# The normalization of six mLSTM heads traced one step later and kept together on VectorE, two blocks scaled at a time

## Chip, cores and metric

The kernel runs on one core of a Trainium2 chip. The core has five engines with a queue of instructions each: TensorE (matmuls; PE in the profile), VectorE (DVE), ScalarE (ACT), GpSimd (POOL) and SyncE (SP), which here only issues DMAs. The metric is the device time of one execution in microseconds (us). The times come from repeated executions, the profile from one more.

## The reference, cut to what matters

The program is a model of two layers in fp32, 512 tokens by 1024 features: dilated window attention and a feed-forward block, then an mLSTM mixer and a feed-forward block, then a last RMS norm. The change lies in the mLSTM mixer. The reference computes it in chunks of 64 tokens:

```python
def mlstm_chunk_step(carry, xs):
    ...
    sm = w_intra * jnp.einsum('bhtd,bhsd->bhts', q, k)
    num = jnp.einsum('bhts,bhsv->bhtv', sm, v) + w_inter[..., None] * jnp.einsum('bhtd,bhdv->bhtv', q, C)
    den = jnp.sum(sm, axis=-1) + w_inter * jnp.einsum('bhtd,bhd->bht', q, n)
    h = num / jnp.maximum(jnp.abs(den), jnp.exp(-m_t))[..., None]
    ...

def mlstm_mixer(xn, w_in, conv_w, conv_b, ig_bias, fg_bias, head_gain, w_out):
    proj = xn @ w_in
    ...
    h = h * lax.rsqrt(jnp.mean(h * h, axis=-1, keepdims=True) + RMS_EPS)
    h = h.reshape(B, S, D_MODEL).astype(xn.dtype) * head_gain.astype(xn.dtype)
    return (h * jax.nn.sigmoid(o_pre)) @ w_out
```

There are 8 heads with keys of 64 and values of 128 features. Each head's output is divided by its denominator, normalized over its 128 features, multiplied by a gain and a gate, and projected.

## The kernel before, in words

**Products.** Weights are fp32 and every projection is done as three matmuls of a high and a low part (`SPLITS`). A chunk of weights, 128 x 1024 values, is loaded by SP into one of three buffers, its high part is made by ScalarE (L209) and its low part by VectorE (L210), each into one of three buffers. `project` takes two chunks for 256 output columns: for each, two times 12 matmuls of 128x512 (L240), in the order high-high, high-low, low-high, so that the third matmul needs the low part. After the second chunk the `evac` of each half runs. `project_tokens` does the same for the values, with 48 matmuls of 128x256 a chunk (L272).

**Steps.** After every chunk `advance()` raises a counter and runs what was deferred to that step (`at_tick`, `defer`; within a step in the order in which it was deferred, that is by head). Counted from `base`, the steps of the mLSTM stage are: 1 to 4 the first values, 5 and 6 query/key columns 0, 7 and 8 columns 2, 9 and 10 values of pair 2, 11 and 12 columns 1, 13 and 14 columns 3, 15 and 16 values of pair 3, and 17 to 24 the four output-gate projections `mo0` to `mo3`. Each query/key projection ends with two evictions `pre` (L1312) and is followed by `convolve`, two chains of four VectorE operations (L1319, L1321) and a Silu.

**Heads.** `HEAD_AT` gives each head a step for its three parts:

- `decay`: one matmul broadcasts a row to a PSUM bank, VectorE adds the mask (L1479), ScalarE takes exponentials.
- `scores`: four pairs of matmuls into two banks, multiplied by the decay on VectorE (L1499).
- `numerators`: 20 matmuls of 128x129 (L1509) into two banks with the tag `o`, of which there are two in all. Column 128 is the denominator. VectorE copies it, takes the larger of its size and a bound, and the reciprocal (L1517 to L1520: five operations on 128x4); ScalarE sums the squares (L1523) into `s2`. Then the normalization: mean and epsilon (L1525), a reciprocal square root by three Newton steps (L189 to L194, eleven operations), a product with the reciprocal (L1527), and four scalings of 128x128 out of PSUM into `yt` (L1530).

As all four blocks of a head fill the two banks, numerators of the next head can begin only when these scalings have read them. For heads 0 to 5 `yt` is then transposed in 32x32 blocks (L1537), and five DMAs on GpSimd's queue carry it through memory into `y` (L1540, L1543). Heads 6 and 7 (`LAST_OUTPUTS`) are turned by matmuls instead, at steps 22 and 23. Numerators are at steps 12, 13, 15, 16, 18, 19, 21 and 21.

**Gates.** The `evac` of `mo` multiplies by the inverse norm (L1575), ScalarE takes the tanh (L1576) and VectorE multiplies into `y` (L1577), for heads 2c and 2c+1 in projection c. After `mo3` all eight `y` are split and the output projection `mwo` begins.

**What sets the order.** A scheduler puts the traced instructions into each engine's queue when the program is compiled: of those whose operands it expects to be ready, the one traced first goes first. On the chip each queue is worked off in that fixed order, and semaphores hold an instruction until its operands are there. `tc.issue_after(x)` adds that all a block traces on the engine of x stands behind x; the helper `behind` does so with the last instruction traced so far on an engine. `tc.add_manual_dep(i, x.name, ...)` of the class `NoSync` puts one instruction i behind x in its queue, without a wait.

Of the kernel before, what the change touches and what calls it, by code (L numbers as in the profile page):

```python
# [15 lines left out]
ALU = mybir.AluOpType  # L16
AX = mybir.AxisListType
P = 128
# [4 lines left out]
TB = SEQ // P  # L23
# [16 lines left out]
LAST_OUTPUTS = {6: 22, 7: 23}  # L40
# [31 lines left out]
def tile_hybrid_dilated_attn_mlstm(  # L72
# [4 lines left out]
    nc = tc.nc  # L77
# [62 lines left out]
    def defer(n, fn):  # L140
        later.append((tick[0] + n, next(order), fn))
# [5 lines left out]
    def run_deferred(due=lambda t: True):  # L147
        while True:
            ready = sorted((e for e in later if due(e[0])), key=lambda e: e[:2])
            if not ready:  # L150
                return
            later.remove(ready[0])
            ready[0][2]()
# [4 lines left out]
    def last_on(engine):  # L158
        for ins in reversed(nc.cur_bb.bb.instructions):
            if ins.engine == engine:  # L160
                return ins
# [22 lines left out]
    def rsqrt_newton(tp_pool, v, n, name, y=None):  # L184

        if y is None:
            y = tp_pool.tile([P, n], F32, tag="rs_y%d" % n, name=name + "_y", bufs=2)
        a = tp_pool.tile([P, n], F32, tag="rs_a%d" % n, name=name + "_a", bufs=2)
        nc.vector.tensor_single_scalar(a.bitcast(I32), v.bitcast(I32), 1, op=ALU.arith_shift_right)  # L189
        nc.vector.tensor_scalar(y.bitcast(I32), a.bitcast(I32), -1, 0x5F3759DF, op0=ALU.mult, op1=ALU.add)  # L190
        for _ in range(3):
            nc.vector.scalar_tensor_tensor(a, y, -0.5, y, op0=ALU.mult, op1=ALU.mult)
            nc.vector.tensor_tensor(a, a, v, op=ALU.mult)
            nc.vector.scalar_tensor_tensor(y, a, 1.5, y, op0=ALU.add, op1=ALU.mult)  # L194
        return y
# [25 lines left out]
    def split_act(hi, lo, src, gain):  # L221

        if gain is None:
            nc.scalar.activation(hi, src, AF.Copy)
            nc.vector.tensor_tensor(lo, src, hi.bitcast(F32), op=ALU.subtract)
        else:
            nc.scalar.activation(hi, src, AF.Copy, scale=gain)
            nc.vector.scalar_tensor_tensor(lo, src, gain, hi.bitcast(F32), op0=ALU.mult, op1=ALU.subtract)
# [16 lines left out]
    def project(pairs, w2d, c0, nk, evac, name, hook=None, ready=()):  # L245

        acc = [acc_tile("%s_%d" % (name, m)) for m in range(2)]
        for ch in range((nk + 3) // 4):
            n = min(4, nk - 4 * ch)
            whl = ready.pop(0) if ready else split_chunk(weight_chunk(w2d, ch, c0, n, "%s_k%d" % (name, ch)))  # L250
            for m in range(2):
                with fenced():
                    multiply(acc[m], whl, pairs, ch, m, nk)
                if 4 * ch + n == nk and hook is None:
                    evac(m, acc[m])
            if 4 * ch + n == nk and hook is not None:
                hook()
                for m in range(2):
                    evac(m, acc[m])
            advance()  # L260
# [85 lines left out]
    with ExitStack() as actx:  # L346
# [64 lines left out]
        def behind(fn, *args, engine=mybir.EngineType.PE):  # L411

            with tc.issue_after(last_on(engine)):
                fn(*args)
# [820 lines left out]
    with ExitStack() as fctx:  # L1235
# [7 lines left out]
        ts = [slice(0, HALF), slice(HALF, SEQ)]  # L1243
# [48 lines left out]
    with ExitStack() as mctx:  # L1292
# [4 lines left out]
        blk = lambda t: t.rearrange("p (b s) -> p b s", b=TB)  # L1297
        FB = 32 * (TB - 1) + H

        def y_tile(k, name):  # L1300
            return mp.tile([P, SEQ], F32, tag="my%d" % k, name=name)
# [94 lines left out]
        for b in range(TB):  # L1396
            ve.scalar_tensor_tensor(fblk[32 * b:32 * b + H], blk(lf)[:, b], bias2[:, 1:2], blk(t0)[:, b],
                                    op0=ALU.add, op1=ALU.add)
# [32 lines left out]
        i = 0  # L1431
# [37 lines left out]
                stacks[2 * p + i] = (ks, qs, ql)  # L1469

        y = [None] * H
        decays, sms, yts = {}, {}, {}

        def decay(hh):
            nm = "m%d" % hh
# [25 lines left out]
        def numerators(hh):  # L1501
            nm = "m%d" % hh
            sm = sms[hh]
            num = [ps.tile([P, 512], F32, tag="o", name=nm + "num", bufs=2) for _ in range(2)]
            nv = lambda qb: num[qb // 2][:, (qb % 2) * 256:(qb % 2) * 256 + P + 1]
            for qb in range(TB):
                for kb in range(qb + 1):
                    o = (qb - kb) * P
                    nc.tensor.matmul(nv(qb), sm[kb][:, o:o + P], vaug[:, kb, hh, :],  # L1509
                                     start=(kb == 0), stop=(kb == qb))  # L1510

            rr = mp.tile([P, TB], F32, tag="rr", name=nm + "rr", bufs=2)
            aa = mp.tile([P, TB], F32, tag="aa", name=nm + "aa", bufs=2)
            s2 = mp.tile([P, TB], F32, tag="s2", name=nm + "s2", bufs=2)
            for t in range(2):
                den = num[t].rearrange("p (a b) -> p a b", a=2)[:, :, P]
                nc.vector.tensor_copy(rr[:, 2 * t:2 * t + 2], den)  # L1517
            nc.vector.scalar_tensor_tensor(aa, rr, -1.0, rr, op0=ALU.mult, op1=ALU.max)
            nc.vector.tensor_tensor(aa, aa, bcol[:, npair:, hh], op=ALU.max)
            nc.vector.reciprocal(rr, aa)  # L1520
            for qb in range(TB):
                junk = mp.tile([P, P], F32, tag="junk", name=nm + "j", bufs=2)
                nc.scalar.activation(junk, nv(qb)[:, :P], AF.Square, scale=rr[:, qb:qb + 1],  # L1523
                                     accum_out=s2[:, qb:qb + 1])
            nc.vector.tensor_scalar(s2, s2, 1.0 / P, EPS, op0=ALU.mult, op1=ALU.add)  # L1525
            rq = rsqrt_newton(mp, s2, TB, nm + "rq")
            nc.vector.tensor_tensor(rr, rr, rq, op=ALU.mult)  # L1527
            yt = mp.tile([P, SEQ], F32, tag="yt", name=nm + "yt", bufs=2)
            for qb in range(TB):
                nc.vector.tensor_scalar(yt[:, qb * P:(qb + 1) * P], nv(qb)[:, :P], rr[:, qb:qb + 1], None,  # L1530
                                        op0=ALU.mult)
            if hh in LAST_OUTPUTS:
                yts[hh] = yt
                return

            turned = npl.tile([P, SEQ], F32, tag="sq", name=nm + "yB", bufs=2)
            nc.vector.transpose(turned.rearrange("p (c i) -> p c i", i=R), yt.rearrange("p (c i) -> p c i", i=R))  # L1537
            d = mdp.tile([P, SEQ], F32, tag="yD", name=nm + "yD", bufs=3)
            for a in range(TB):
                nc.gpsimd.dma_start(d.rearrange("(f j) (q a i) -> a j q f i", f=4, q=TB, a=4)[a],  # L1540
                                    turned[R * a:R * (a + 1)].rearrange("p (q f i) -> p q f i", q=TB, f=4))
            y[hh] = y_tile(hh, "y%d" % hh)
            nc.gpsimd.dma_start(y[hh], d)  # L1543

        def outputs(hh):
            tp = ps.tile([P, 512], F32, tag="t", name="m%dyT" % hh, bufs=1)
            for qb in range(TB):
                transpose_into(tp, qb, yts[hh][:, qb * P:(qb + 1) * P])
            y[hh] = y_tile(hh, "y%d" % hh)
            nc.scalar.activation(y[hh], tp, AF.Copy)  # L1550

        def at_tick(t, fn):
            defer(base + t - tick[0], fn)
# [3 lines left out]
        for hh, ts in enumerate(HEAD_AT):  # L1557
            for t, fn in zip(ts, (decay, scores, numerators)):
                at_tick(t, lambda hh=hh, fn=fn: fn(hh))
        for hh, t in LAST_OUTPUTS.items():  # L1560
            at_tick(t, lambda hh=hh: outputs(hh))
        for pr, cs in ((2, (0, 2)), (3, (1, 3))):
# [8 lines left out]
        for c in range(KC // 2):  # L1571
# [5 lines left out]
                nc.vector.scalar_tensor_tensor(y[j], t, 1.0, y[j], op0=ALU.add, op1=ALU.mult)  # L1577
            project(pair, w_in2, 2 * D + c * 256, KC, evac, "mo%d" % c)
        run_deferred()
        for j in range(H):  # L1580
            split_act(ypair[0][j], ypair[1][j], y[j], hg[:, j:j + 1])
    out_project(ypair, mlstm_w_out[0], KC, "mwo")
# [3 lines left out]
    with ExitStack() as fctx:  # L1586
# [22 lines left out]
        for n in (1, 0):  # L1609
            for tb in range(TB):  # L1610
                t = ht[tb, n] = hp.tile([P, SEQ], F32, tag="h", name="ht%d_%d" % (tb, n), bufs=KC + 1)
# [65 lines left out]
        t = ht[TB - 1, 0][:, 256:]  # L1677
# [3 lines left out]
        for acc, tb, cs in tiles:  # L1681
# [10 lines left out]
            else:  # L1692
# [3 lines left out]
                                               op0=ALU.mult, op1=ALU.add)  # L1696
# [33 lines left out]
```

## Time and profile before

| what | value |
|---|---|
| time before, median of 3 runs (lowest to highest) | 1416.81 us (1416.67 to 1419.73) |
| the profiled execution's own time | 1416.74 us |
| its span, first to last instruction | 1415.0 us |
| mean granted TensorE clock | 0.999 |
| numerators of head 0 begin on TensorE | 924.2 us |
| numerators of head 7 begin | 1010.8 us |
| first matmul of `mwo` | 1021.4 us |

A row of a timeline gives start, duration (both us), engine, line, operation, output and inputs by the program's names, shape and count; in brackets is the idle time of the engine before it, and what ended it. `m1yt` is `yt` of head 1, `m1num` its numerators, `m1s` the sums of squares (or scores, where TensorE writes them), `m1e` the decayed scores, `m1rq` the Newton steps. Rows of the view of waits name who waited, for whom, the total in us, how often, and the longest. A row on a tile gives shortest, median and longest duration in ns and the starts of the first and the last instruction. In a row of busy sums each engine has its busy time, and x counts instructions. TensorE's instructions overlap: one starts before the one ahead of it has ended, so the distance of starts is what one costs.

### The profile page before, as it was taken

To read this page: it belongs to the slowest core of one execution; us is meant where nothing else is said; L and a number is where in the kernel's file an instruction comes from. 1 tells how busy PE (TensorE), PEld (TensorE's weight loads), DVE (VectorE), ACT (ScalarE), POOL (GpSimd) and SP (SyncE) were. 2 spreads that over 40 slices of the span, in tenths; PEclk is the share of its full clock that TensorE was granted. 3 is DMA by queue.
4 is the path that set the end of the run, shared out by engine and by line. 5 is a ranking of instruction groups with operands and counts; after the bars stand their busy time and mean duration, and the time that the engine had idled before them with its cause. 6 is when DMAs were issued, how large, how long until landed. Compare 5 with 4: busy or idle time off the path is not lost. (4 is left out here: it accounts for less than half of the span.)

```text
span 1415.0 us, 20843 instructions
## 1 busy us (share of the span) xinstructions
PE 1401.2 (99%) x8094; PEld 1235.3 (87%) x8094; DVE 1046.7 (74%) x1798; ACT 634.2 (45%) x1061; POOL 125.3 (9%) x197
## 2 busy tenths in 40 slices
PE   9999999999999999999999999999999999999997
PEld 7888888888888888999998988888888899999876
DVE  7867557566567398877777868998758888778874
ACT  5333224224225244444574343785534344447433
POOL 1011011002003000000000000112101230000011
PEclk9999999999999999999999999999999999999999
DMA  6346235335435434233334433324333562333542
GB/s 196 101 113 205 77 105 177 114 98 141 149 98 130 160 111 143 69 112 120 109 99 136 135 120 92 89 76 117 93 105 104 156 182 80 120 120 107 162 119 104
DMA packets 134650, 171.27 MB, mean 121 GB/s; under 512 B 8276, under 2 KB 110996, under 8 KB 134552
## 3 DMA queue, kind: packets, MB, share of 16 engines
q1 hardware_dynamic: 124848, 140.99, 32.2%
q0 software_dynamic: 8048, 27.84, 7.5%
q8 instruction: 63, 1.03, 0.3%
q10 hardware_dynamic: 1656, 1.12, 0.2%
q14 instruction: 35, 0.29, 0.1%
HBM read 154.19 MB, written 15.73 MB: 120 GB/s over the span
## 5 line engine op out<-in xcount | busy, mean ns | idle before, releaser
L240 PE MATMUL f1j<-n_h,f1j_h 128*128 128x512 f32 x96 | 37.5, 390 | 0.0
L240 PE MATMUL f0j<-n_h,f0j_h 128*128 128x512 f32 x96 | 37.5, 390 | 0.0
L240 PE MATMUL f0j<-n_h,f0j_l 128*128 128x512 f32 x96 | 37.4, 389 | 0.0
L240 PE MATMUL f1j<-n_h,f1j_l 128*128 128x512 f32 x96 | 37.4, 389 | 0.0
L240 PE MATMUL f0j<-n_l,f0j_h 128*128 128x512 f32 x96 | 37.3, 389 | 0.0
L240 PE MATMUL f1j<-n_l,f1j_h 128*128 128x512 f32 x96 | 37.3, 389 | 0.0
L1356 POOL MEMSET gates_h<- 128x1024 f32 x1 | 1.0, 957 | 382.3 <-PE fo L1249 382.3
L1249 PE MATMUL fo<-f0hh,f0w_h 128*128 128x512 f32 x80 | 31.2, 390 | 0.0
L1249 PE MATMUL fo<-f0hl,f0w_h 128*128 128x512 f32 x80 | 31.2, 390 | 0.0
L1249 PE MATMUL fo<-f0hh,f0w_l 128*128 128x512 f32 x80 | 31.1, 389 | 0.0
L1600 POOL DMA_DIRECT2D hD<-hB x32 | 20.6, 650 | 96.6 <-DVE hB L1597 96.0
L539 DVE TENSOR_TENSOR rot<-rot,sinr 32x1024 f32<-32x1024 f32 x24 | 28.9, 1206 | 0.0
L240 PE MATMUL mo<-n_h,mo_k_h 128*128 128x512 f32 x64 | 25.3, 396 | 0.0
L240 PE MATMUL mo<-n_h,mo_k_l 128*128 128x512 f32 x64 | 25.2, 394 | 0.0
L240 PE MATMUL mqk<-n_h,mqk_k_h 128*128 128x512 f32 x64 | 25.1, 392 | 0.0
L240 PE MATMUL mwo<-yo_l,mwo_k_h 128*128 128x512 f32 x64 | 25.1, 392 | 0.0
L240 PE MATMUL mo<-n_l,mo_k_h 128*128 128x512 f32 x64 | 25.1, 392 | 0.0
L240 PE MATMUL mqk<-n_l,mqk_k_h 128*128 128x512 f32 x64 | 25.1, 392 | 0.0
L240 PE MATMUL awo<-ao_h,awo_k_h 128*128 128x512 f32 x64 | 25.1, 392 | 0.0
L240 PE MATMUL mwo<-yo_h,mwo_k_l 128*128 128x512 f32 x64 | 25.0, 391 | 0.0
L240 PE MATMUL mqk<-n_h,mqk_k_l 128*128 128x512 f32 x64 | 25.0, 390 | 0.0
L240 PE MATMUL awo<-ao_h,awo_k_l 128*128 128x512 f32 x64 | 25.0, 390 | 0.0
(2249 smaller groups left out, 5359.4 us busy)
## 6 DMA issues: line engine op xcount, KB each, us to landing
f0j_w<-in_ffn_w_in_dram SPq DMA_DIRECT2D x28, 512.0 KB, 4.0
f1j_w<-in_ffn_w_in_dram SPq DMA_DIRECT2D x28, 512.0 KB, 4.0
f0w_w<-in_ffn_w_out_dram SPq DMA_DIRECT2D x10, 512.0 KB, 3.8
f1w_w<-in_ffn_w_out_dram SPq DMA_DIRECT2D x10, 512.0 KB, 4.4
awo_k_w<-in_attn_w_out_dram SPq DMA_DIRECT2D x8, 512.0 KB, 7.6
mv_k_w<-in_mlstm_w_in_dram SPq DMA_DIRECT2D x8, 512.0 KB, 3.7
mqk_k_w<-in_mlstm_w_in_dram SPq DMA_DIRECT2D x8, 512.0 KB, 3.7
mo_k_w<-in_mlstm_w_in_dram SPq DMA_DIRECT2D x8, 512.0 KB, 3.8
```

The costliest lines, as they stand in the source:

```text
L240: nc.tensor.matmul(acc, whl[a][:, k, m * P:(m + 1) * P], pairs[b][kk], start=(kk == 0 and (a, b) == SPLITS[0]), stop=(kk == nk - 1 and (a, ...
L539: nc.vector.tensor_tensor(sh, sh, sinr.unsqueeze(1).to_broadcast([R, 2, SEQ]), op=ALU.mult)
L1249: nc.tensor.matmul(acc, w[a_][:, k, m * P:(m + 1) * P], b[b_][k], start=(fresh and k == 0 and (a_, b_) == SPLITS[0]), stop=(k == 1 and (a_ ...
L1356: nc.gpsimd.memset(gh.bitcast(F32), 0.0)
L1600: nc.gpsimd.dma_start(hD[k // 4].rearrange("(b i) x -> i b x", i=R)[:, :, c0:c0 + R], t[R * a_:R * (a_ + 1)])
```

## The change

The normalization becomes a function of its own. For heads 0 to 5 it is deferred to the step after the numerators and traced through `behind`, so that all its VectorE instructions stand behind the last VectorE instruction traced before it. For heads 6 and 7 it is called at the end of `numerators` as before. The four scalings of 128x128 with a scalar per partition become two products of two blocks each (128x256) with `rr` broadcast along the features. The last of these two is noted in `ends` for every head. When all deferred parts have run, `keep_together` puts the 40 VectorE instructions traced after each of these ends behind it in the queue (fewer where fewer are left; the splits of `y` and all of `mwo` are traced later and are not among them). The transpose and the DMAs follow the scaling as before and so move with it.

```diff
+        ends = []
+
+        def keep_together():
+            ins = [i for i in nc.cur_bb.bb.instructions if i.engine == mybir.EngineType.DVE]
+            for end in ends:
+                at = next(k for k in range(len(ins)) if ins[k] is end)
+                for i in ins[at + 1:at + 1 + 40]:
+                    tc.add_manual_dep(i, end.name, mybir.DependencyInfo(
+                        mybir.DependencyClass.NoSync, mybir.DependencyReason.DATA), reason="behind")
...
+            norms[hh] = num, rr, s2
+            if hh in LAST_OUTPUTS:
+                normalize(hh)
+
+        def normalize(hh):
+            nm = "m%d" % hh
+            num, rr, s2 = norms[hh]
             nc.vector.tensor_scalar(s2, s2, 1.0 / P, EPS, op0=ALU.mult, op1=ALU.add)
             rq = rsqrt_newton(mp, s2, TB, nm + "rq")
             nc.vector.tensor_tensor(rr, rr, rq, op=ALU.mult)
             yt = mp.tile([P, SEQ], F32, tag="yt", name=nm + "yt", bufs=2)
-            for qb in range(TB):
-                nc.vector.tensor_scalar(yt[:, qb * P:(qb + 1) * P], nv(qb)[:, :P], rr[:, qb:qb + 1], None,
-                                        op0=ALU.mult)
+            for t in range(2):
+                two = slice(2 * t, 2 * t + 2)
+                nc.vector.tensor_tensor(blk(yt)[:, two], num[t].rearrange("p (a b) -> p a b", a=2)[:, :, :P],
+                                        rr[:, two].unsqueeze(2).to_broadcast([P, 2, P]), op=ALU.mult)
+            ends.append(last_on(mybir.EngineType.DVE))
...
+            if hh not in LAST_OUTPUTS:
+                at_tick(ts[2] + 1, lambda hh=hh: behind(normalize, hh, engine=mybir.EngineType.DVE))
...
         run_deferred()
+        keep_together()
         for j in range(H):
```

More of the change, by code (lines that the diff above doesn't have):

```diff
@@ L1471, in tile_hybrid_dilated_attn_mlstm @@
         y = [None] * H
-        decays, sms, yts = {}, {}, {}
+        decays, sms, norms, yts = {}, {}, {}, {}
+        ends = []
[6 more added lines that the diff above has]
+                        mybir.DependencyClass.NoSync, mybir.DependencyReason.DATA), reason="behind")
         def decay(hh):
```

## The prediction

> **What bounds the kernel now.** I read the busy table first, then TensorE's waits between 895 and 1030 us (the mLSTM heads), then the busy sums of that stretch.
>
> ```profile
> span 1415.0 us, 20843 instructions
> PE   1401.2 (99%) x8094; PEld 1235.3 (87%) x8094; DVE 1046.7 (74%) x1798; ACT 634.2 (45%) x1061; POOL 125.3 (9%) x197
> ```
> ```profile
> PE m2num L1509 <- DVE m1yt L1530: 1.1, 1, 1.1
> PE m1nb L1477 <- ACT m0e L1487: 0.4, 1, 0.4
> PE m3s L1497 <- DVE m3e L1499: 0.2, 1, 0.2
> ```
> ```profile
> sum 130.00, PE 128.22 PEld 110.44 DVE 112.10 ACT 91.57 POOL 28.83; mean PE 14.25 PEld 12.27 DVE 12.46 ACT 10.17 POOL 3.20
> ```
>
> TensorE has work in 1401 of 1415 us, and in the 130 us from 895 to 1025 it idles 1.8 us. So shorter work on VectorE gains nothing by itself; the change can win back those waits, 1.7 us at most, and it can lose whatever it takes from TensorE's supply. That supply is the split weights: every chunk needs its low part (L210, on VectorE) before the chunk's third matmul. So I looked at how early the splits are made.
>
> ```profile
> L210 DVE TENSOR_TENSOR mqk_k_l<-mqk_k_w,mqk_k_h x4: 1212/1220/1226, 902.4 to 919.2; 128x1024 fp32r<-128x1024 f32 x4
> L272 PE MATMUL mv<-mv_k_l,n_h x32: 278/283/363, 942.4 to 958.2; 128*128 128x256 f32 x32
> L210 DVE TENSOR_TENSOR mv_k_l<-mv_k_w,mv_k_h x2: 1217/1218/1218, 926.1 to 940.2; 128x1024 fp32r<-128x1024 f32 x2
> L210 DVE TENSOR_TENSOR mo_k_l<-mo_k_w,mo_k_h x8: 1204/1216/1225, 946.3 to 1001.1; 128x1024 fp32r<-128x1024 f32 x8
> ```
>
> The first value chunk here is split at 926.1 and used at 942.4: 16 us early, because the scheduler fills gaps on VectorE with any ready instruction, whatever its place in the trace. The change takes exactly that freedom away.
>
> ```profile
> 931.09 0.16 DVE L1525 TENSOR_SCALAR m0s<-m0s 128x4 f32<-128x4 f32 x1
> 932.48 0.16 DVE L193 TENSOR_TENSOR m0rq_a<-m0rq_a,m0s 128x4 f32<-128x4 f32 x1
> 934.26 0.42 DVE L1499 SCALAR_TENSOR_TENSOR m2e<-m2s,m2e 128x256 f32<-128x256 f32 x1
> 934.60 0.15 DVE L193 TENSOR_TENSOR m0rq_a<-m0rq_a,m0s 128x4 f32<-128x4 f32 x1
> 935.73 1.12 DVE L1530 TENSOR_SCALAR m0yt<-m0num,m0rr 128x128 f32<-128x128 f32 x4
> 937.37 0.70 DVE L1537 STREAM_TRANSPOSE m0yB<-m0yt 128x512 f32<-128x512 f32 x1
> 942.55 0.65 DVE L1312 TENSOR_TENSOR pre<-mqk,n2rbc 128x512 f32<-128x512 f32 x1
> 943.12 1.14 DVE L1499 SCALAR_TENSOR_TENSOR m3e<-m3s,m3e 128x512 f32<-128x512 f32 x2
> 944.25 0.17 DVE L1525 TENSOR_SCALAR m1s<-m1s 128x4 f32<-128x4 f32 x1
> 945.81 0.48 DVE L1319 TENSOR_SCALAR conv<-pre,cols 128x512 f32<-128x512 f32 x1
> 947.49 0.74 DVE L1321 SCALAR_TENSOR_TENSOR conv<-pre,cols,conv 128x512 f32<-128x512 f32 x1
> 948.15 0.15 DVE L192 SCALAR_TENSOR_TENSOR m1rq_a<-m1rq_y 128x4 f32<-128x4 f32 x1
> 954.10 1.13 DVE L1530 TENSOR_SCALAR m1yt<-m1num,m1rr 128x128 f32<-128x128 f32 x4
> ```
>
> **What the change does to the order.** A head's normalization is 13 small operations (one on s2, eleven of Newton, one on rr), the scaling and the transpose. Before, they are interleaved with long operations: head 0 from 931.09 to 936.85, head 1 from 944.25 to 955.2. After, `keep_together` puts the 40 VectorE instructions traced next behind the end of the scaling. By the trace order (step n is the n-th chunk since `base`) these 40 hold the next one or two splits. And `behind` puts the block after the last VectorE instruction traced so far, which is at step 14 (head 1) the eviction `pre` of the query/key chunk just computed, and at step 20 (head 5) the last `y` of output-gate pair 1. There the order becomes: TensorE finishes a product, eviction, whole normalization, and only then the split that TensorE's next chunk needs.
>
> **Length of the block.** The first eight small operations of head 0 ran alone, from 931.09 to 932.48 + 0.16: 0.2 us each. Thirteen take 2.6. The scaling of two blocks does not occur before; its nearest row is the 128x256 tensor operation out of PSUM, 0.34 from its start to the next (934.26 to 934.60), so 0.7 for two against 1.12 for four. Bounds: half of the 1.12 (0.56) and twice 0.42 plus 0.3 for the broadcast operand (1.1); I take 0.7. Block: 3.3 us, and the head's PSUM banks come free at its end, the first one 0.35 earlier. VectorE loses about 1 us a head in unfilled gaps and gains 0.4; where TensorE waits for nothing from it, that costs 0, hidden under matmuls.
>
> **Head 0 (step 13).** The block starts about where it did, 931, and ends at 934.3, 2.5 us sooner; numerators 1 move forward and fill TensorE while the split of the next chunk (now after transpose and two score products) is made by about 937. +0.4.
>
> **Head 1 (step 14).** The two evictions, the block, then scores 3, `convolve(3)` and only then the first split of the value pair.
>
> ```profile
> 941.28 0.40 PE L240 MATMUL mqk<-n_h,mqk_k_l 128*128 128x512 f32 x1
> 941.51 0.39 PE L1497 MATMUL m3s<-qs,ks 128*128 128x512 f32 x1
> 942.33 0.28 PE L272 MATMUL mv<-mv_k_h,n_h 128*128 128x256 f32 x1
> 953.50 0.28 PE L272 MATMUL mv<-mv_k_h,n_h 128*128 128x256 f32 x1
> 954.86 2.47 PE L1509 MATMUL m2num<-vaug,m2e 128*128 128x129 f32 x20 [1.08 <-DVE m1yt L1530]
> ```
>
> The query/key product ends at 941.5 now, 942 then. Eviction to 942.7, block to 946.0. TensorE has four score matmuls (0.8, from 941.51 to 942.33) and stands from 943 to 945.7, when the first bank frees: 2.7. Then numerators 2 (2.47 less the overlap of the last: 2.3), two score pairs and a bank of decay (0.7) carry it to 948.7. VectorE after 946.0: transpose 0.65, four score products 1.7 (1.1 for the first two, 0.34 and about 0.2), eight convolution operations (each starts some 0.07 before the one ahead ends, 947.49 to 948.15: two of 0.4, six of 0.67: 4.8), the split 1.15: 954.3. All of them are ready and traced before the split, so they go first. Second wait 954.3 - 948.7 = 5.6. Together 8.3. Bounds: if the split is picked right after the block it ends at 947.2, under numerators 2, and only 2.7 is lost; if squares or evictions slip in as well, 10.
>
> **Heads 2 to 4 (steps 16, 17, 19).** They are placed behind a split or a stack of queries, not behind a product. The block, transpose, two score products and a split take 3.3 + 0.65 + 1.1 + 1.15 = 6.2; the cover is numerators of the next head (2.3) and the half chunk or more still on TensorE (24 matmuls, 0.23 apart from 941.28 to 941.51: 5.5 us a chunk). 0; without the cover of the chunk 3.9 each.
>
> **Head 5 (step 20).** Behind the last `y` of pair 1.
>
> ```profile
> 972.85 0.68 DVE L1575 TENSOR_TENSOR og<-mo,n2rbc 128x512 f32<-128x512 f32 x1
> 974.31 0.69 DVE L1577 SCALAR_TENSOR_TENSOR y<-og,y 128x512 f32<-128x512 f32 x1
> 980.44 0.16 DVE L1517 COPY m4rr<-m4num 128x2 f32<-128x2 f32 x1 [0.34 <-PE m4num L1509]
> 982.91 0.35 DVE L1525 TENSOR_SCALAR m4s<-m4s 128x4 f32<-128x4 f32 x1 [1.70 <-ACT m4j L1523]
> ```
>
> From the product's end T: gate to `y` 1.46 (972.85 to 974.31) plus 0.1, `y` 0.65, block to the first bank 2.95: T + 5.2. TensorE has four score matmuls and two of the next chunk, 1.3: a wait of 3.9. Numerators 6 last to T + 7.5, the split comes at T + 8.4: 0.9 more. Together 4.8.
>
> **Heads 6 and 7 (step 21)** are not moved, but their followers are held too, and the second split of pair 2 stands behind both. From numerators to s2 it takes 2.5 (980.44 to 982.91). Copies wait for that split, so s2 of head 6 comes at T + 10.9 and its first bank at T + 13.8. TensorE has one chunk (5.5 and 0.5 of scores, to T + 14.4), numerators 7 to T + 16.7; s2 at T + 19.2, block to T + 22.5, split T + 23.7. Two matmuls and four transposes cover 0.9: 6.1 lost. Bounds 4 (head 6's copies go first) and 8.
>
> ```profile
> 1000.46 0.71 DVE L1537 STREAM_TRANSPOSE m5yB<-m5yt 128x512 f32<-128x512 f32 x1
> 1012.17 0.69 DVE L1577 SCALAR_TENSOR_TENSOR y<-og,y 128x512 f32<-128x512 f32 x1 [0.31 <-DMA y<-m5yD]
> ```
>
> **Queues.** The transposes' five GpSimd DMAs a head go out up to a step later. Round trip: `m5yB` ends at 1001.17, its `y` is read at 1012.17, 11 us; y5 would then be there at T + 22, and is first asked for after pair 2 ends (later than T + 29): 0. Without that slack it is a wait of VectorE and up to 3. Weight loads on SP start as buffers free, and three buffers hold them: 0.
>
> **Sum.** 0.4 + 8.3 + 4.8 + 6.1 = 19.6, less the waits for `m1yt` and `m3e` (1.1 + 0.2): +18.3. The profiled execution took 1416.74 (span 1415.0 and 1.7 around it), the median of the runs is 1416.81: no correction. Forecast 1435 us, own range 1430 to 1440.
>
> **The rivals.**
> (a) *Splits come first.* Were each split picked as soon as a block ends, head 1 costs 2.7 and head 5 3.9: 0.4 + 2.7 + 3.9 + 6.1 - 1.3 = 11.8, so 1428.5. For it: at 926.1 a split did slip between convolution steps. Against: two convolutions are then ready at once and leave no gap.
> ```profile
> 1.52 3.98 PE L108 MATMUL idle<-idle_w,ones_r 128*128 128x512 f32 x10 [1.52 <-DVE idle_w L103]
> ```
>
> (b) *The matmuls after a long wait are slow.* The first ten, after idling, took 3.98 us where ten take 0.23 x 10 + 0.16 = 2.5.
>
> That is 1.5 us more a wait; after four waits of 2.7 to 6 us it adds 6: 1441. Against: shorter waits here show nothing. The Trainium skill ("TensorE: Matmul & The Clock Gate", the part on the clock gate) says that an idle window of about 3.4 us halves TensorE's clock until about 3.4 us of work have passed; by it the three longer waits would each cost about 1.7 us, an estimate. The row at 1.52 agrees in its pace, though the clock column there reads 1.00.
> (c) *Every block is exposed*, heads 2 to 4 too: three times 3.9, 11.7 more: 1447. For it: VectorE is busy 112 of 130 us, so a block that starts late has little slack. Against: TensorE's chunk covers it.
> (d) *Not slower: banks first.* What paces the heads is two PSUM banks held until the scaling; blocks of 3.3 instead of 5.8 to 11 us free them sooner, the 1.3 us of waits vanish, and the held splits are still in time: 1415.4. This decides if VectorE reaches a split more than 1.2 us before its chunk; the slack now is 13 us and more. Against: at steps 14 and 20 the block itself waits for TensorE's last product, and no slack survives that. Nor does the change do what it says if earlier-traced work still slips into the block, which lengthens it by 1 to 2 us a head and lies in (c).
>
> **How the numbers follow.** Forecast 0.45, (a) 0.16, (b) 0.14, (c) 0.11, (d) 0.11, faster by over 0.2% 0.03 (only if work outside this stretch moves too, since the waits in it are worth 1.7 us). A change of 0.2%, 2.8 us, is about what a measurement of this kernel can tell from none. Faster 0.03, same 0.11, slower 0.86. The range 1425 to 1448 holds the forecast, (a), (b), (c): 0.86.
>
> **What would show it.** After: TensorE waits of several us for L210 low parts (`mv_k_l` once, `mo_k_l` twice) and for `m1yt`, `m5yt`, `m6yt`; the first value split after 950 instead of 926.1; blocks of 3 to 4 us without another instruction inside; the first `mwo` matmul 15 to 20 us later. Wrong if the value split still precedes the block of head 1, if TensorE's idle time in the stage stays under 3 us, or if the granted clock falls after the waits (b).

## The result, and the profile after

| | before | after |
|---|---|---|
| time, median of 5 runs (lowest to highest) | 1416.81 us (1416.63 to 1419.73) | 1442.07 us (1440.23 to 1444.46) |
| ratio after to before | | 1.0174, 95% interval 1.0161 to 1.0188 |
| the profiled execution | 1416.74 us, span 1415.0 | 1443.55 us, span 1441.7 |
| mean granted TensorE clock | 0.999 | 0.990 |
| numerators of head 0 begin | 924.2 us | 927.0 us |
| first matmul of `mwo` | 1021.4 us | 1048.9 us |

The change costs 25.3 us. In the profiled execution the stretch from head 0's numerators to the first `mwo` matmul grew from 97.2 to 121.9 us, by 24.7. Behind it the two programs need about the same (393.6 and 392.8 us to the end). The 2.8 us by which head 0 begins later are lost around 755 us, far ahead of the change. In the traces of the experiments head 0 begins at 924.1 to 925.3 us, so none of them lost as much there. Whether the other four executions after the change did is not known, as they left no trace.

The busy sums of this stretch, after and then before. A row gives the window, its length, then busy time and count of PE, PEld, DVE, ACT and POOL, the mean granted clock (the clock that TensorE was given, as a share of its full one), the DMA share and GB/s.

```profile
927.00:1048.90 121.90, 103.80 (x559) 88.56 (x558) 89.09 (x254) 68.87 (x177) 24.31 (x34) 0.92 0.31 83
```
```profile
924.20:1021.40 97.20, 95.80 (x556) 82.21 (x555) 83.58 (x260) 67.88 (x176) 24.38 (x34) 1.00 0.36 93
```

Two things grew. TensorE stands still for 18.1 us (121.9 - 103.8) instead of 1.4, so 16.7 more. And it is busy for 8.0 us longer (103.8 - 95.8) with the same work, while the granted clock falls from 1.00 to 0.92. Where it stands still is in TensorE's waits of the profile after, from 895 to 1060 us:

```profile
PE m7yT L306 <- DVE m7yt L1548: 5.3, 1, 5.3
PE mv L272 <- DVE mv_k_l L210: 5.0, 1, 5.0
PE m6num L1519 <- DVE m5yt L1548: 3.6, 1, 3.6
PE mo L240 <- ACT mo_k_h L209: 1.4, 1, 1.4
PE m2num L1519 <- DVE m1yt L1548: 1.3, 1, 1.3
PE mqk L240 <- DVE mqk_k_l L210: 0.4, 1, 0.4
```

The 1.4 is for a high part: ScalarE makes `mo_k_h` late, at 947.05 to 948.09, behind its other work. Before, the longest wait was 1.1. VectorE's timeline around head 1's block shows where the 5.0 comes from:

```profile
946.45 0.69 DVE L1312 TENSOR_TENSOR pre<-mqk,n2rbc 128x512 f32<-128x512 f32 x1 [1.58 <-PE mqk L240]
947.06 0.16 DVE L1542 TENSOR_SCALAR m1s<-m1s 128x4 f32<-128x4 f32 x1
...
949.63 0.76 DVE L1548 TENSOR_TENSOR m1yt<-m1num,m1rr 128x256 f32<-128x256 f32 x2
...
950.90 0.70 DVE L1556 STREAM_TRANSPOSE m1yB<-m1yt 128x512 f32<-128x512 f32 x1
...
955.63 2.73 DVE L1321 SCALAR_TENSOR_TENSOR conv<-pre,cols,conv 128x512 f32<-128x512 f32 x4
958.28 1.22 DVE L210 TENSOR_TENSOR mv_k_l<-mv_k_w,mv_k_h 128x1024 fp32r<-128x1024 f32 x1
```

VectorE waits for TensorE's product, evicts it, and works through the whole block without anything in between, as the change wants: 3.3 us from 947.06 to the end of `m1yt` (950.39) instead of the 11 of before. But the split that TensorE needs next stands behind the transpose, the score products and the convolutions and begins at 958.28; before, the value splits were made at 926.1 and 940.2. TensorE's timeline at the same place:

```profile
959.55 0.58 PE L272 MATMUL mv<-mv_k_l,n_h 128*128 128x256 f32 x1 [5.02 <-DVE mv_k_l L210]
...
960.15 0.41 PE L272 MATMUL mv<-mv_k_h,n_h 128*128 128x256 f32 x1
960.36 0.42 PE L272 MATMUL mv<-mv_k_l,n_h 128*128 128x256 f32 x1
```

Behind the wait the value matmuls start 0.21 us apart; before, the same ones are 0.12 apart:

```profile
942.45 0.28 PE L272 MATMUL mv<-mv_k_l,n_h 128*128 128x256 f32 x1
942.57 0.28 PE L272 MATMUL mv<-mv_k_h,n_l 128*128 128x256 f32 x1
```

The granted clock goes with it, in windows of 5 us around the waits of head 1 and behind those of heads 5 and 7:

```profile
945.00:950.00 5.00, 2.50 (x11) 1.51 (x9) 3.10 (x16) 4.20 (x7) 0.00 (x0) 0.97 0.20 52
950.00:955.00 5.00, 4.33 (x24) 4.17 (x24) 3.78 (x9) 0.80 (x2) 2.90 (x4) 0.68 0.27 43
955.00:960.00 5.00, 0.45 (x2) 0.45 (x3) 5.00 (x8) 3.09 (x4) 0.04 (x1) 0.66 0.09 13
960.00:965.00 5.00, 5.00 (x31) 5.00 (x31) 4.87 (x10) 4.29 (x6) 2.62 (x3) 0.66 0.56 157
965.00:970.00 5.00, 5.00 (x44) 5.00 (x43) 2.95 (x17) 4.40 (x18) 0.00 (x0) 1.00 0.35 105
...
1015.00:1020.00 5.00, 5.00 (x23) 4.49 (x22) 2.65 (x10) 1.50 (x8) 2.81 (x4) 0.70 0.61 147
...
1030.00:1035.00 5.00, 3.29 (x9) 2.54 (x10) 4.83 (x10) 0.60 (x1) 0.00 (x0) 0.50 0.23 54
```

The clock is lowered after the stops: 0.66 to 0.68 behind the waits of head 1, 0.70 behind that of head 5, 0.50 behind that of head 7. In the windows from 960 to 970 TensorE is busy all the time, but does 31 matmuls in the first and 44 in the second. So the loss has two parts, the waits (16.7) and the slow matmuls behind them (8.0). Together they are the 24.7 of the stretch.

### The profile page after: what moved, and what is told of

Read it like the earlier page. It is cut to its first block, busy times and chain, and to the rows that moved or that the text cites. A ratio compares the mean times of both kernels' runs of the same rounds, so it can differ in the third digit from the quotient of the medians.

```text
span 1441.7 us, 20822 instructions
## 1 busy us (share of the span) xinstructions
PE 1411.1 (98%) x8094; PEld 1244.0 (86%) x8094; DVE 1049.6 (73%) x1782; ACT 634.3 (44%) x1061; POOL 125.2 (9%) x197
## 3 DMA queue, kind: packets, MB, share of 16 engines
q10 hardware_dynamic: 1656, 1.12, 0.2%
## 5 line engine op out<-in xcount | busy, mean ns | idle before, releaser
L240 PE MATMUL awo<-ao_l,awo_k_h 128*128 128x512 f32 x64 | 24.9, 390 | 0.0
```

The costliest lines, as they stand in the source:

```text
L240: nc.tensor.matmul(acc, whl[a][:, k, m * P:(m + 1) * P], pairs[b][kk], start=(kk == 0 and (a, b) == SPLITS[0]), stop=(kk == nk - 1 and (a, ...
```

## The experiments

Three theories were to be told apart. Theory 1: the loss comes from what `keep_together` holds back, the splits above all. Theory 2: the place of the block (one step later, behind an eviction) costs by itself. Theory 3, beside theory 1: a part of the loss is the granted clock. All ratios are to the kernel before, run on the same chip with the same batch of kernels (1417.08 us for the first four, 1417.63 for the last four; 1416.81 beside the change). The three medians of the kernel before differ by 0.8 us, so a difference between medians of two batches carries about that much.

| experiment | time, median (lowest to highest) | ratio, 95% interval |
|---|---|---|
| e1, no hold | 1417.86 (1417.20 to 1418.16) | 1.0004 (0.9994 to 1.0013) |
| e2, weight splits exempt | 1426.24 (1424.16 to 1428.70) | 1.0064 (1.0050 to 1.0077) |
| e3, only the scaling changed | 1418.34 (1417.33 to 1418.64) | 1.0005 (0.9996 to 1.0014) |
| e4, heads 6 and 7 hold nothing | 1434.69 (1433.66 to 1435.47) | 1.0122 (1.0108 to 1.0136) |
| e5, zeros in the waits | 1436.37 (1436.09 to 1436.91) | 1.0135 (1.0120 to 1.0150) |
| e6, splits and evictions exempt | 1418.27 (1417.33 to 1420.34) | 1.0007 (0.9997 to 1.0016) |
| e7, held, but in the same step | 1467.23 (1465.48 to 1467.33) | 1.0352 (1.0335 to 1.0370) |
| e8, only the splits held | 1443.90 (1443.71 to 1444.13) | 1.0188 (1.0172 to 1.0203) |

The stretch from head 0's numerators to the first `mwo` matmul, measured in each of these traces as in the two rows above (length, what TensorE stands still in it, what it is busy, its mean clock):

| trace | length | idle | busy | clock |
|---|---|---|---|---|
| before | 97.2 | 1.4 | 95.8 | 1.00 |
| after | 121.9 | 18.1 | 103.8 | 0.92 |
| e1 | 97.8 | 1.5 | 96.4 | 1.00 |
| e2 | 107.5 | 7.6 | 100.0 | 0.97 |
| e4 | 114.2 | 13.2 | 101.0 | 0.96 |
| e5 | 117.6 | 4.6 | 113.0 (15.6 of it zeros) | 1.00 |
| e6 | 98.2 | 2.5 | 95.7 | 1.00 |
| e7 | 146.4 | 36.7 | 109.7 | 0.88 |
| e8 | 125.2 | 21.1 | 104.1 | 0.90 |

### e1: the later step and the scaling without the hold

```diff
         run_deferred()
-        keep_together()
```

> The changed kernel without the call of keep_together: the later step, the place behind the last VectorE instruction and the scaling of two blocks stay, nothing is held. Theory 1 (the held weight splits starve TensorE): no wait of TensorE on a low part over 1 us, the first value split before 935 us again, 1417 to 1420 us. Theory 2 (the place behind the last eviction of a product holds the PSUM banks, and with them TensorE): the waits on m1yt and m5yt stay at 2.7 and 3.9 us, 1422 to 1426. Theory 3 (half clock after long waits adds about 6 us) gives no half clock in the heads' stretch under theory 1 and perhaps one under theory 2.

The loss is gone: 1417.86, the same as before. VectorE's timeline shows what the scheduler makes of the block when it is free:

```profile
939.49 1.23 DVE L210 TENSOR_TENSOR mv_k_l<-mv_k_w,mv_k_h 128x1024 fp32r<-128x1024 f32 x1 [0.50 <-ACT mv_k_h L209]
...
944.78 0.17 DVE L1542 TENSOR_SCALAR m1s<-m1s 128x4 f32<-128x4 f32 x1
...
947.47 1.22 DVE L210 TENSOR_TENSOR mo_k_l<-mo_k_w,mo_k_h 128x1024 fp32r<-128x1024 f32 x1
...
954.49 0.75 DVE L1548 TENSOR_TENSOR m1yt<-m1num,m1rr 128x256 f32<-128x256 f32 x2
```

The block still stands behind the eviction, but it is open again: 10.5 us from 944.78 to 955.24, with a split in the middle of it and both value splits ahead of it (the second at 939.49, the first at 927.07). TensorE waits for `m1yt` once, and little:

```profile
PE m2num L1519 <- DVE m1yt L1548: 1.0, 1, 1.0
```

A block three times as long costs nothing. Theory 2 falls: the later step and the place cost nothing that can be measured as long as nothing is held, and without the hold the 25 us are not there.

### e2: the low parts of the weights exempt from the hold

```diff
+    low_parts = set()
...
         nc.vector.tensor_tensor(lo[:, :n], raw[:, :n], hi[:, :n].bitcast(F32), op=ALU.subtract)
+        low_parts.add(last_on(mybir.EngineType.DVE).name)
...
                 for i in ins[at + 1:at + 1 + 40]:
+                    if i.name in low_parts:
+                        continue
```

> The changed kernel with the low parts of the weights (L210) taken out of the 40 held instructions; all else is held as before. Theory 1: the waits on mv_k_l (5.0 us) and the long one before m7yT vanish, what is left are the waits on the blocks of heads 1 and 5: 1420 to 1426 us. Theory 2: most of the loss stays, 1432 or more. In both, a split made early must have a chunk of TensorE's work to cover the blocks.

The time came out 0.2 us above what theory 1 gave, and not with its waits. TensorE's longest waits in this trace:

```profile
PE m7yT L308 <- DVE m7yt L1552: 3.9, 1, 3.9
PE m4num L1523 <- DVE m3yt L1552: 1.9, 1, 1.9
```

No wait for a low part is left in the list, so that part is shown: with the splits let past, 16 of the 25 us are gone. The 3.9 before `m7yT` was not foreseen. The likely reason is the evictions of `mo`, which are held behind the blocks of heads 6 and 7 too, so that the PSUM accumulators are not free for TensorE's next chunk. VectorE makes them only when the block of head 7 is done:

```profile
1024.40 1.28 DVE L1600 TENSOR_TENSOR og<-mo,n2rbc 128x512 f32<-128x512 f32 x2
```

e6 tests it. The windows around the wait for `m3yt`:

```profile
977.20:980.60 3.40, 1.53 (x12) 1.14 (x11) 3.30 (x9) 0.00 (x0) 0.00 (x0) 1.00 0.86 249
980.60:984.00 3.40, 3.40 (x18) 3.40 (x17) 2.26 (x6) 0.63 (x1) 2.76 (x4) 0.50 0.61 162
```

A wait of 1.9 us, in a window of 3.4 in which TensorE works for 1.53, is followed by 3.4 us at clock 0.50, in which half of the work of 3.4 us is done. So, as an estimate from these two rows, a wait of 1.9 us cost about 1.7 more than itself here.

### e3: only the scaling of two blocks

The kernel before with this edit alone:

```diff
-            for qb in range(TB):
-                nc.vector.tensor_scalar(yt[:, qb * P:(qb + 1) * P], nv(qb)[:, :P], rr[:, qb:qb + 1], None,
-                                        op0=ALU.mult)
+            for t in range(2):
+                two = slice(2 * t, 2 * t + 2)
+                nc.vector.tensor_tensor(blk(yt)[:, two], num[t].rearrange("p (a b) -> p a b", a=2)[:, :, :P],
+                                        rr[:, two].unsqueeze(2).to_broadcast([P, 2, P]), op=ALU.mult)
```

> The kernel before with the scaling of two blocks at a time as its only edit. The two operations take 0.75 us instead of 1.12 (as in the changed kernel's rows), so the banks come free 0.4 us earlier a head. All theories: within 0.2% of before, 1415.5 to 1417.5; the wait before the numerators of head 2 shrinks from 1.1 to about 0.7 us. A rival that the broadcast operand costs: over 1418.

The median lies above the range that was expected, and in what was named as a sign that the broadcast costs (over 1418). The ratio's interval holds 1, though, so no cost is shown, and no gain. The pair takes 0.75 where four took 1.12. Yet the wait that it was to shorten is 1.0, not the 0.7 expected:

```profile
PE m2num L1509 <- DVE m1yt L1531: 1.0, 1, 1.0
```

Some 0.4 us less on VectorE is nothing here. A likely reason is that the scaling comes at the end of an open block (944.68 to 955.15 for head 1) whose length the neighbours set.

### e4: heads 6 and 7 hold nothing

```diff
-            ends.append(last_on(mybir.EngineType.DVE))
+            if hh not in LAST_OUTPUTS:
+                ends.append(last_on(mybir.EngineType.DVE))
```

> The changed kernel with the hold for heads 0 to 5 only; heads 6 and 7 hold nothing back. Prediction's step for heads 6 and 7: 6.1 us, and with theory 3 one half-clock stretch less (1.5 to 2 us): 1433 to 1436 us, the wait before m7yT under 1 us. If heads 6 and 7 cost nothing by themselves: 1442.

1442.07 - 1434.69 = 7.4 us, between two batches, are the share of heads 6 and 7. In the waits the 5.3 has gone and the 3.6 is as it was:

```profile
PE m6num L1519 <- DVE m5yt L1548: 3.6, 1, 3.6
...
PE m7yT L306 <- ACT mwo_k_h L209: 0.3, 1, 0.3
```

So the term of heads 6 and 7 could be taken off by itself, without changing the waits of the heads before. In the stretch 4.9 us less are idle (18.1 to 13.2) and 2.8 less busy (103.8 to 101.0): the wait, and slow matmuls that went with it. The windows at head 5's wait and behind it hold a surprise:

```profile
1010.00:1015.00 5.00, 2.93 (x24) 2.77 (x24) 4.79 (x14) 0.00 (x0) 1.62 (x3) 1.00 0.09 13
1015.00:1020.00 5.00, 4.96 (x22) 4.12 (x23) 3.26 (x10) 1.83 (x9) 1.32 (x2) 1.00 0.81 229
```

The same wait of 3.6 us for `m5yt`, from 1008.1 to 1011.7, leaves the clock at 1.00 here; after the change it was 0.70 behind it.

### e5: zeros in the waits

TensorE is given matmuls with a matrix of zeros to do where it would wait; they add zeros to sums that are being built, and leave them as they are. 70 of 128x256 stand in the value chunk of head 1, 16 of 128x512 in each chunk of `mo2`.

```diff
+                if (a, b) == SPLITS[1]:
+                    for _ in range(fill):
+                        nc.tensor.matmul(acc, zero[0], pairs[b][kk], start=False, stop=False)
...
+                            if name == "mv3" and kk == 0 and m == 0 and i == 0 and (a, b) == SPLITS[0]:
+                                for _ in range(70):
+                                    nc.tensor.matmul(acc[m][:, :256], zero[0], whl[0][:, k, :], start=False,
+                                                     stop=False, skip_group_check=True)
```

> The changed kernel with matmuls by a matrix of zeros added to the accumulators where TensorE stands idle: 70 of 128x256 in the first chunk of the last value pair (8.4 us), 16 of 128x512 in each chunk of output-gate pair 2 (3.6 us each); they change no sum. TensorE has 15.6 us more work, laid into waits of 2.7 + 5.0, 3.6 and 5.6 us. Theory 3 (half clock after idling costs about 6 us of the 25): the four half-clock stretches go, 1436 to 1439 us although work was added. If the slow clock costs nothing beyond the waits: 1442 to 1445.

More work, less time: 1436.37, 5.7 us under the change (6.5 when each is taken against the kernel before in its own batch). The zeros cost TensorE about 15.6 us (70 x 0.12 + 32 x 0.227), and it still stands still for 4.6 us of the stretch, together 20.2 against 18.1 after. What was won is the clock:

```profile
924.20:1041.80 117.60, 113.02 (x662) 97.13 (x661) 88.28 (x254) 68.94 (x177) 24.39 (x34) 1.00 0.32 86
...
960.00:965.00 5.00, 5.00 (x43) 4.92 (x42) 3.05 (x14) 3.98 (x19) 0.00 (x0) 1.00 0.37 116
```

1.00 over the whole stretch, and 43 matmuls of 128x256 from 960 to 965 where the change did 31. Theory 3 is shown. Its size is less sharp. Without the zeros TensorE's own work takes 97.4 us here (113.0 - 15.6), against 103.8 after the change and 95.8 before, so 6.4 of the 8.0 come back with the clock. The stretch itself is shorter by 4.3 (121.9 to 117.6), as 2.1 of that go to zeros and standing still. The rest of what lies between the two profiled executions is the 2.8 around 755 us. So some 6 to 8 of the 25 us are the clock's.

### e6: evictions and gate products exempt as well

e2, and the same mark after three more of VectorE's operations, the evictions `pre` and `og` and the product into `y`:

```diff
                 nc.vector.tensor_tensor(pre[m][:, 3:], acc, rbc, op=ALU.mult)
+                low_parts.add(last_on(mybir.EngineType.DVE).name)
...
                 nc.vector.tensor_tensor(t, acc, rbc, op=ALU.mult)
+                low_parts.add(last_on(mybir.EngineType.DVE).name)
                 nc.scalar.activation(t, t, AF.Tanh, scale=0.5)
                 nc.vector.scalar_tensor_tensor(y[j], t, 1.0, y[j], op0=ALU.add, op1=ALU.mult)
+                low_parts.add(last_on(mybir.EngineType.DVE).name)
```

> As the kernel with free splits, but the evictions of the projections (pre, og and the product into y) are taken out of the 40 held instructions as well; only work of the heads themselves is held. Theory 1, widened (what starves TensorE is any held instruction that TensorE's next chunk needs: a low part, or an eviction that frees an accumulator): the wait before m7yT (3.9 us) and the half clock after it go, 1417 to 1421 us. If the held score products, convolutions and stacks are what costs: 1424 to 1427, as before this edit.

1418.27, the same as before. Only short waits are left in the stretch, this the longest, and the clock is 1.00 in it:

```profile
PE m4num L1524 <- DVE m3yt L1553: 1.4, 1, 1.4
```

The rest of the 40 may be held, then, at no cost that can be measured, if what feeds TensorE (splits) and what frees its accumulators (evictions) goes past. It also gains nothing. Which of the three exempted operations counts was not taken apart. Nor does e6 show that a closed block is free of cost, for what may go past also slips into the blocks. Head 5's block:

```profile
999.95 0.16 DVE L1547 TENSOR_SCALAR m5s<-m5s 128x4 f32<-128x4 f32 x1
...
1001.30 1.23 DVE L211 TENSOR_TENSOR mo_k_l<-mo_k_w,mo_k_h 128x1024 fp32r<-128x1024 f32 x1
...
1003.31 0.68 DVE L1601 TENSOR_TENSOR og<-mo,n2rbc 128x512 f32<-128x512 f32 x1
...
1004.10 0.76 DVE L1553 TENSOR_TENSOR m5yt<-m5num,m5rr 128x256 f32<-128x256 f32 x2
```

It takes 4.9 us, and those of heads 1, 3, 4 and 7 take 5.4, 8.7, 5.3 and 9.5; only heads 0, 2 and 6 keep the 3.3 of the change.

### e7: the hold without the later step

Every head is normalized at the end of `numerators`, and held there.

```diff
-            if hh in LAST_OUTPUTS:
-                normalize(hh)
+            normalize(hh)
...
-            if hh not in LAST_OUTPUTS:
-                at_tick(ts[2] + 1, lambda hh=hh: behind(normalize, hh, engine=mybir.EngineType.DVE))
```

> The changed kernel without the later step: each head is normalized at the end of its numerators as in the kernel before, and the 40 are held behind every head. Theory 1: the splits now wait for numerators, 2.5 us of denominators and squares and the block, with one chunk less in hand, some 5 to 7 us at each of heads 0 to 5, and half clock after most: 1455 to 1480 us. If the later step is itself what costs: faster than the changed kernel, under 1435.

Twice the loss: 49.6 us. Now the other heads are waited for as well:

```profile
PE m7yT L306 <- DVE m7yt L1547: 5.3, 1, 5.3
...
PE m4s L1507 <- DVE m4e L1509: 4.7, 1, 4.7
PE m3num L1519 <- DVE m2yt L1547: 4.7, 1, 4.7
...
PE m5num L1519 <- DVE m4yt L1547: 4.1, 1, 4.1
```

The later step is thus the half of the change that helps, given the hold. After the change the waits for `m4e` and `m4yt` were 0.3 each, as TensorE has more of a chunk to do while the block runs; here they are 4.7 and 4.1. The step halves a loss that the hold brings in.

### e8: only the splits held

e2 with the condition turned round: `if i.name not in low_parts: continue`.

> The reverse of the kernel with free splits: of the 40 only the low parts of the weights are held. Theory 1: the split comes right after the block, before the convolutions, so head 1 costs its first wait alone (2.7, rival (a) of the prediction) and heads 5 to 7 about what they did: 1428 to 1436 us. If the order among all held instructions does it: under 1422.

A miss: 1443.9, as slow as the full hold. VectorE's timeline tells why at head 1:

```profile
943.76 0.16 DVE L1546 TENSOR_SCALAR m1s<-m1s 128x4 f32<-128x4 f32 x1
...
953.06 0.76 DVE L1552 TENSOR_TENSOR m1yt<-m1num,m1rr 128x256 f32<-128x256 f32 x2
953.73 1.22 DVE L211 TENSOR_TENSOR mv_k_l<-mv_k_w,mv_k_h 128x1024 fp32r<-128x1024 f32 x1
```

With everything else free to slip in, the block of head 1 is 10 us long again, and the split that must wait for its end is nearly as late as if it had waited for convolutions behind a short block: it begins 11.1 us after the end of the query/key product, against 12.0 after the change. The waits get other names. TensorE's queue was planned with scores ahead of the chunk, and they wait for `ks` until 951.25, when the low part would not have been there either. The blocks of the other heads are 3.3 to 4.5 us long, and heads 6 and 7 cost more than after the change:

```profile
PE m4s L1511 <- DVE ks L1465: 5.4, 1, 5.4
PE m7yT L308 <- DVE m7yt L1552: 5.3, 1, 5.3
PE m7num L1523 <- DVE m6yt L1552: 4.6, 1, 4.6
```

The 4.6 is new. The last six matmuls of numerators 6 stand behind most of a chunk in TensorE's queue here (at 1015.72), so the block of head 6 ends only at 1022.33, and the low parts that TensorE needs next are made only behind the block of head 7, from 1031.85.

For head 1 the expectation counted only what was taken out of the hold, and forgot that the hold on the rest is what made the block short. For heads 6 and 7 it took over the waits of another order. With e2 it says: hold all but the splits, and 9 us are lost; hold the splits alone, and 26 are.

## Why the prediction came out as it did

The forecast was 1435 in a range of 1425 to 1448, with the sign right; the median was 1442.07, 7 us above the forecast and next to rival (b), 1441. It lies inside the wide range, which was drawn to hold the rivals too, but outside the forecast's own range of 1430 to 1440. One of the signs that the forecast named for being wrong did appear: the granted clock falls after the waits.

- **Length of the block.** 3.3 forecast, 3.3 measured; the pair of scalings 0.75 for 0.7.
- **Head 0.** +0.4 forecast; the wait for `mqk_k_l` is 0.4.
- **Head 1.** 8.3 forecast (2.7 for the banks, 5.6 for the split). Measured 1.4 + 1.3, parted by two output-gate matmuls that the forecast did not have, then 5.0: 7.7. That the first part fits so well is luck. By the forecast's own rows TensorE is out of work from 942.3 and not from 943, so its 2.7 should have been 3.4, and the two matmuls that were not foreseen took just 0.7. The 1.4 of it is also for a high part that ScalarE made late, and not for a bank. The second wait is for `mv_k_l` behind the convolutions, as worked out. Rival (a), the split right after the block, falls with that row.
- **Heads 2 to 4.** 0 forecast, 0.3 for each of two waits measured; rival (c) falls. e7 shows what the cover was worth: without the later step `m2yt` and `m4yt` are waited for 4.7 and 4.1 us.
- **Head 5.** 3.9 for the bank and 0.9 for the split forecast; 3.6 and 0 measured. The 3.6 is in part luck: the bank came 6.1 us after the product's end and not 5.2, and TensorE had four more matmuls to do, which made up for it. The second wait did not come because numerators 6, with two score pairs in between and at the slow pace, took 3.9 us and not 2.3, which gave the split time.
- **Heads 6 and 7.** 6.1 forecast; 5.3 measured, and 7.4 in time by e4, with the slow matmuls behind it.
- **Sum of the waits.** 18.3 net forecast, 16.7 measured. The mechanism and its places were right, and the sizes nearly so.
- **The clock.** This is the term that was mis-sized. The forecast set it to nothing and priced it only in rival (b): 6 us with a chance of 0.14, "shorter waits here show nothing". Measured are 8.0 by the busy sums, of which e5 wins back 6.4. With 1.6 less of waits this covers most of the 7 us between forecast and result. So the price in rival (b) was about right, and its place outside the sum was the mistake: waits of 2.7 to 6 us had been forecast by the sum itself, and the row that the forecast shows behind an idle TensorE (at 1.52 us) took 3.98 us where ten matmuls take 2.5. The rule of the Trainium skill quoted there ("TensorE: Matmul & The Clock Gate", the part on the clock gate) agrees with the traces in size, clock 0.50 after a stop. But it speaks of an idle window, and in e2 TensorE was busy for 1.53 of the 3.4 us before the slow stretch.
- **Rival (d), not slower.** It asked that 1.2 us of a slack of 13 and more survive. They didn't: the split moved from 926.1 to 958.28. e1 and e6 show that without the held splits and evictions nothing is lost, and also that the 1.3 us of waits to be won back were not won in any of them: in e1 the wait for `m1yt` is still 1.0, and in e6 it is gone, but others of 1.4 and 0.6 came.
- **Queues.** 0 forecast for SP's and GpSimd's DMAs; no wait of TensorE in the stretch after the change names one.

Left open: why the wait for `m1yt` stays at 1.0 in e1 and e3, whatever the scaling costs, was not followed up; and the stretch around 755 us was not tried by itself.

## What to carry to other kernels

When an order is pinned on one engine, price what is pinned behind it, not what is kept together: list which of the held instructions feed the engine that bounds the kernel or free its buffers, and let those pass (e6 against the change: 24 us). A long but open sequence off the critical path cost nothing here (e1), and no run gained from a shorter one. Where a forecast has the bounding TensorE wait for some microseconds, add the slow matmuls that may follow to the sum: here they were about half as much again as the waits (8.0 to 16.7).

## What was not expected of the hardware

The granted clock can fall after windows in which TensorE is only thinly used and not idle: in e2 after 3.4 us with 1.53 us of matmuls and no wait over 1.9; after the change behind two waits of 1.4 and 1.3 us (2.50 of 5 us busy from 945 to 950). And the same wait does not always cost it: 3.6 us for `m5yt` left 1.00 in e4 and 0.70 after the change. What decides was not settled. The stretch ahead of the change that cost the profiled execution 2.8 us may be of this kind. Here are its busy sums before and after, from 752 to 765 us, with 1.0 and 1.9 us idle and the clock at 1.00 and 0.87:

```profile
752.00:765.00 13.00, 11.99 (x86) 11.26 (x87) 11.88 (x15) 7.56 (x11) 0.00 (x0) 1.00 0.53 163
```
```profile
752.00:765.00 13.00, 11.11 (x77) 10.68 (x76) 11.40 (x13) 7.13 (x11) 0.00 (x0) 0.87 0.49 163
```

Useless work can pay, then: 102 matmuls by zeros, 15.6 us of TensorE's time, made the changed program some 6 us shorter.
